# Low parts of streamed weights made by ScalarE and an accumulating GpSimd DMA instead of a VectorE subtraction

## The chip, the cores and the metric

One Trainium2 chip; the kernel runs on 1 core, so there is one span and one granted TensorE clock per run. The metric is the device time of one execution in microseconds (us). Times are medians of several executions; the profile is one further execution with a time of its own.

## The reference, cut to what matters

Two layers of a decoder trunk on 512 tokens of 1024 features. Each layer is an FFN half-step, a mixer, and another FFN half-step; layer 0 has the indexed sparse attention (mixer A), layer 1 the gated MLP (mixer B).

```python
def swiglu(x, w_in, w_out):
    gate, up = jnp.split(x @ w_in, 2, axis=-1)
    return (jax.nn.silu(gate) * up) @ w_out
...
    for i in range(DEPTH):
        kind, j = i % N_MIXERS, i // N_MIXERS
        h = h + 0.5 * swiglu(rmsnorm(h, norm_g[i, 0]), ffn_w_in[i, 0], ffn_w_out[i, 0])
        hn = rmsnorm(h, norm_g[i, 1])
        if kind == 0:
            y = mixer_a(hn, a_w_in[j], a_w_out[j], rel_table)
        elif kind == 1:
            y = mixer_b(hn, b_w_in[j], b_b_in[j], b_ln_g[j], b_ln_b[j], b_w_sp[j], b_b_sp[j], b_w_out[j])
```

D_MODEL is 1024, D_FF 2816, and mixer B's inner width 3072. Everything is float32, about 200 MB of weights are read once (the last FFN's output weights partly twice), and each weight is used for all 512 tokens.

## The kernel before, in words

**Precision by splitting.** TensorE multiplies in the fp32r format. To keep float32 accuracy every operand is a sum of a high part (rounded to fp32r) and a low part (what is left). A product of weight and activation is three matmuls into one PSUM bank (`mul3`, lines 217 to 219): high weight by high activation, high weight by low activation, low weight by high activation. The low weight is thus first needed by the third matmul of a piece.

**The weight stream.** A piece is one 128x128 block of weights. All pieces lie in DRAM in the order of their use, eight to a load of 512 KB (`in_wst`). `WeightStream` keeps three queues going. `_load_to` starts loads on the SP queue into four `raw` buffers. `_convert_to` takes four pieces (a conversion): ScalarE (ACT) copies `raw` into `whi` (line 92), and `lo_engine` writes `wlo = raw - whi` (line 93). `lo_engine` is VectorE (DVE) as a rule; while DVE is busy with a row of small dependent operations, the code sets it to GpSimd (POOL): in the first FFN from its third column pair to its seventh, and in the middle of mixer A. `take` hands out pieces and first asks for conversions up to AHEAD = 5 conversions ahead, each in one of 6 buffers. `background` holds small DVE tasks, some of which are started after each conversion.

**The order of work.** There is no scheduler. Each engine runs its instructions in the order in which the code is written and waits on semaphores, so an instruction that waits holds all that stand behind it on the same engine. DMAs issued by POOL go into one queue (q0 in the profile), those by SP into another (q1).

**The stages.** An FFN first multiplies by `ffn_w_in` (`group` for the first four column blocks, then `single` for one block at a time), forms `yh` and `yl` on ACT and DVE, and then multiplies by `ffn_w_out` and adds to `H`. In the first FFN the hook `behind(k)` prepares the next block of activations after every four pieces (ACT writes `xh` and a square, POOL adds the square to `sqacc`). After the fourth block it also calls `bias_rows`: TensorE makes a small table of relative position biases, DVE copies it to `rows`, and POOL issues one DMA that writes 2560 KB of copies of it to DRAM (`dist`, line 339). Mixer A reads them later (`tb`). At its start mixer B loads `bias`, `wT`, `bs` and three small vectors by POOL DMAs, and POOL masks `wT` when it has landed (line 627). In the last FFN the output columns come in two halves of 256 tokens, so each weight is used by matmuls of half the width and the weights pass twice as fast. While the second half runs, POOL normalizes the first half (`hg`, line 792) and issues its four output DMAs.

Of the kernel before, what the change touches and what calls it, by code (L numbers as in the profile page):

```python
# [12 lines left out]
F32 = mybir.dt.float32  # L13
F32R = mybir.dt.float32r
I32 = mybir.dt.int32
AF = mybir.ActivationFunctionType
ALU = mybir.AluOpType
PSUM = bass.MemoryType.PSUM

P = 128  # L20
D = 1024
S = 512
# [20 lines left out]
CONV = 4  # L43
LOAD = 8
# [3 lines left out]
SPACE = 8  # L48


class WeightStream:

    AHEAD = 5
    LOADS_AHEAD = 3

    def __init__(self, nc, pool, dram):
# [24 lines left out]

    def _convert_to(self, n):
        while self.converted < min(n, N_PIECES // CONV):
            c = self.converted
            i, part = divmod(c * CONV, LOAD)
            self._load_to(i + self.LOADS_AHEAD + (part > 0))
            src = self.raw[i][:, part * P:(part + CONV) * P]
            hi = self.pool.tile([P, CONV * P], F32R, tag="whi", bufs=self.AHEAD + 1, name=f"whi{c}")  # L90
            lo = self.pool.tile([P, CONV * P], F32R, tag="wlo", bufs=self.AHEAD + 1, name=f"wlo{c}")
            self.nc.scalar.activation(hi, src, AF.Copy)  # L92
            self.lo_engine.tensor_tensor(lo, src, hi.bitcast(F32), op=ALU.subtract)  # L93
            self.conv[c] = (hi, lo)
            self.conv.pop(c - self.AHEAD - 1, None)
            self.converted += 1
            for _ in range(min(self.pops, len(self.background))):
                self.background.pop(0)()

    def take(self, *specs):  # L100
        at = len(self.specs)
        c, off = divmod(at, CONV)
        assert off + len(specs) <= CONV
        self._convert_to(c + min(self.AHEAD, c + 1))
        self.specs += specs
# [10 lines left out]
def tile_trunk(ctx: ExitStack, tc, specs_out, xT, wst, gT, rel, onehot, bu, bv, lng, lnb, wspT, bsp, out):  # L116
# [12 lines left out]
    def uname(s):  # L129
        counter[0] += 1  # L130
        return f"{s}_{counter[0]}"
# [106 lines left out]
    def split(src, hi, lo):  # L238
        nc.scalar.activation(hi, src, AF.Copy)  # L239
        nc.vector.tensor_tensor(lo, src, hi.bitcast(F32), op=ALU.subtract)  # L240

    def ffn(layer, which, finish, hooks=None, parts=1):


        NJ = DFF // P
        half = NJ // 2
        with tc.tile_pool(name=uname("ffn"), bufs=1) as fp:

            def spec_in(k, c):
# [2 lines left out]
            def activate(psg, psu, rb):  # L252
                gs = fp.tile([P, S], F32, tag="gs", bufs=2, name=uname("gs"))
                us = fp.tile([P, S], F32, tag="us", bufs=2, name=uname("us"))
                sg = fp.tile([P, S], F32, tag="sg", bufs=2, name=uname("sg"))
                a = fp.tile([P, S], F32, tag="a", bufs=2, name=uname("a"))
                nc.vector.tensor_tensor(gs, psg, rb, op=ALU.mult)
                nc.scalar.activation(sg, gs, AF.Silu)
                nc.vector.tensor_tensor(us, psu, rb, op=ALU.mult)
                nc.vector.tensor_tensor(a, sg, us, op=ALU.mult)  # L260
                yh = fp.tile([P, S + SPACE], F32R, tag="yh", bufs=half + 1, name=uname("yh"))[:, :S]
                yl = fp.tile([P, S + SPACE], F32R, tag="yl", bufs=half + 1, name=uname("yl"))[:, SPACE // 2:S + SPACE // 2]
                split(a, yh, yl)
                return yh, yl

# [5 lines left out]
            for hf in range(2):  # L271
# [10 lines left out]
                def activate_one():  # L282
                    if pend and rb[0] is not None:
                        Y.append(activate(*pend.pop(0), rb[0]))

                for p in range(p0 + len(pend), p0 + half):
                    tag = "aux" if (p // 2) % 2 else "acc"
# [20 lines left out]
                for at in range(0, S, n):  # L308
                    s = slice(at, at + n)
# [433 lines left out]
    with tc.tile_pool(name="bias", bufs=1) as bp:  # L743
        table, dist = load_table(), []
        ffn(0, 0, into(1), {k: lambda k=k: behind(k) for k in range(KD)})
    mixer_a(dist[0], 2)
    ffn(0, 1, into(3))
    ffn(1, 0, into(4))
    mixer_b(5)

# [101 lines left out]
```

## Time and profile before

| what | value |
| --- | --- |
| time, median of 3 executions | 2156.6 us (2156.14 to 2157.45) |
| the profiled execution's own time | 2156.59 us |
| its span, first to last instruction | 2154.8 us |
| mean granted TensorE clock | 0.998 |
| TensorE (PE) busy | 2135.0 us, 99% |
| VectorE busy | 1141.3 us, 53% |
| ScalarE busy | 752.8 us, 35% |
| GpSimd busy | 131.9 us, 6% |

The profiled execution stands at the median, and its span is 1.8 us shorter than its time. The engines work beside each other, so the busy times do not add up; a busy PE row says that matmuls follow each other without a gap, not how fast they are.

### The profile page before, as it was taken

The numbers are of one execution on the slowest core, as the hardware profiler recorded it, in microseconds if no ns is written. First come the engines' busy times: TensorE is split into PE (matmuls) and PEld (weight loads), VectorE is DVE, ScalarE is ACT, GpSimd is POOL, SyncE is SP. The second block draws the span as 40 slices with busy tenths as digits, with TensorE's granted clock in tenths as the row PEclk, the third lists the DMA queues.
The fourth block names the chain that finished last, engine by engine and source line by source line (L and its number), as shares of the span: only waits on it lengthen the run. The fifth ranks groups of instructions, "written<-read, shape, count | busy, mean of one in ns | idle before, by whom it ended". The sixth has DMA issues, their size and how long they took to land.

```text
span 2154.8 us, 25553 instructions
## 1 busy us (share of the span) xinstructions
PE 2135.0 (99%) x9816; PEld 1768.0 (82%) x9816; DVE 1141.3 (53%) x1968; ACT 752.8 (35%) x1317; POOL 131.9 (6%) x122
## 2 busy tenths in 40 slices
PE   8999999999999999999999999999999999999998
PEld 7788888888888888888888888888888888888888
DVE  6443444696656434445543444555846466533456
ACT  4322333444443322333332333333423243322344
POOL 3300000143200000000000000000000000000002
PEclk9999999999999999999999999999999999999999
DMA  6532223232122332223322232422222223222234
GB/s 181 133 98 97 94 94 98 83 108 83 60 88 98 98 98 94 95 87 107 99 97 89 98 98 88 148 88 90 97 89 91 85 88 108 97 91 96 98 123 132
DMA packets 60426, 214.67 MB, mean 100 GB/s; under 512 B 7232, under 2 KB 8320, under 8 KB 60176
## 3 DMA queue, kind: packets, MB, share of 16 engines
q1 hardware_dynamic: 57136, 203.97, 29.0%
q0 software_dynamic: 2624, 8.54, 1.9%
q8 instruction: 77, 1.26, 0.2%
q10 hardware_dynamic: 544, 0.52, 0.1%
q14 instruction: 45, 0.37, 0.1%
HBM read 208.29 MB, written 4.72 MB: 99 GB/s over the span
## 4 chain that ended last, share of the span: by engine, by line
PE 95%; DMA 3%; issue 1%; POOL 1%; DVE 0%; ACT 0%; POOLq 0%; SPq 0%; ACTq 0%
PE acc L217 16%; PE acc L219 16%; PE acc L218 16%; PE aux L219 12%; PE aux L217 12%; PE aux L218 12%; DMA raw<-in_wst 2%; PE aux L636 1%; PE aux L638 1%; PE acc L638 1%; PE acc L636 1%; PE aux L637 1%; PE acc L637 1%; PE aux L688 1%; PE acc L556 1%
## 5 line engine op out<-in xcount | busy, mean ns | idle before, releaser
L92 ACT ACTIVATE whi<-raw 128x512 fp32r<-128x512 f32 x768 | 466.6, 626 | 752.7 <-PE acc L218 357.0
L93 DVE TENSOR_TENSOR wlo<-raw,whi 128x512 fp32r<-128x512 f32 x698 | 474.5, 700 | 448.7 <-ACT whi L92 448.5
L217 PE MATMUL acc<-xh,whi 128*128 128x512 f32 x1048 | 417.9, 399 | 7.5 <-ACT xh L174 6.5
L219 PE MATMUL acc<-xh,wlo 128*128 128x512 f32 x1048 | 408.9, 390 | 0.6 <-POOL wlo L93 0.6
L218 PE MATMUL acc<-xl,whi 128*128 128x512 f32 x1048 | 408.8, 390 | 0.0
L217 PE MATMUL aux<-xh,whi 128*128 128x512 f32 x720 | 280.2, 389 | 0.9 <-ACT whi L92 0.9
L219 PE MATMUL aux<-xh,wlo 128*128 128x512 f32 x720 | 280.2, 389 | 0.6 <-POOL wlo L93 0.6
L218 PE MATMUL aux<-xl,whi 128*128 128x512 f32 x720 | 280.1, 389 | 0.0
L217 PEld LDWEIGHTS acc<-xh,whi 128*128 128x128 f32 x1048 | 197.3, 188 | 50.1 <-ACT xh L174 6.5
L219 PEld LDWEIGHTS acc<-xh,wlo 128*128 128x128 f32 x1048 | 197.0, 188 | 42.4 <-POOL wlo L93 1.1
L218 PEld LDWEIGHTS acc<-xl,whi 128*128 128x128 f32 x1048 | 197.3, 188 | 41.9 <-issue 1.4
L217 PEld LDWEIGHTS aux<-xh,whi 128*128 128x128 f32 x720 | 135.2, 188 | 29.4 <-ACT whi L92 1.4
L219 PEld LDWEIGHTS aux<-xh,wlo 128*128 128x128 f32 x720 | 135.2, 188 | 29.1 <-POOL wlo L93 1.1
L218 PEld LDWEIGHTS aux<-xl,whi 128*128 128x128 f32 x720 | 135.2, 188 | 28.2
L219 PE MATMUL aux<-yh,wlo 128*128 128x512 f32 (+1 forms) x396 | 146.3, 370 | 0.0
L219 PE MATMUL acc<-yh,wlo 128*128 128x512 f32 (+1 forms) x396 | 146.3, 369 | 0.0
L217 PE MATMUL aux<-yh,whi 128*128 128x512 f32 (+1 forms) x396 | 146.0, 369 | 0.0
L217 PE MATMUL acc<-yh,whi 128*128 128x512 f32 (+1 forms) x396 | 146.0, 369 | 0.0
L218 PE MATMUL acc<-yl,whi 128*128 128x512 f32 (+1 forms) x396 | 145.7, 368 | 0.0
L218 PE MATMUL aux<-yl,whi 128*128 128x512 f32 (+1 forms) x396 | 145.7, 368 | 0.0
L93 POOL TENSOR_TENSOR wlo<-raw,whi 128x512 fp32r<-128x512 f32 x70 | 93.4, 1347 | 166.6 <-ACT whi L92 120.5
L240 DVE TENSOR_TENSOR yl<-a,yh 128x512 fp32r<-128x512 f32 x88 | 62.5, 710 | 61.5 <-ACT yh L239 61.5
(211 smaller groups left out, 2559.0 us busy)
## 6 DMA issues: line engine op xcount, KB each, us to landing
raw<-in_wst SPq DMA_DIRECT2D x383, 512.0 KB, 3.4
dist<-rows POOLq DMA_DIRECT2D x1, 2560.0 KB, 57.0
h<-in_xT SPq DMA_DIRECT2D x8, 256.0 KB, 6.6
tb<-dist POOLq DMA_DIRECT2D x8, 256.0 KB, 3.4
bias<-in_bv POOLq DMA_DIRECT2D x1, 1536.0 KB, 7.2
out<-hg POOLq DMA_DIRECT2D x4, 256.0 KB, 3.3
raw<-in_wst SPq DMA_DIRECT2D x2, 256.0 KB, 3.6
wT<-in_wspT POOLq DMA_DIRECT2D x1, 512.0 KB, 8.2
```

The lines of the kernel that those rows point to most:

```text
L92: self.nc.scalar.activation(hi, src, AF.Copy)
L93: self.lo_engine.tensor_tensor(lo, src, hi.bitcast(F32), op=ALU.subtract)
L217: mm(ps, wh, xh, start=first, stop=False)
L218: mm(ps, wh, xl, start=False, stop=False)
L219: mm(ps, wl, xh, start=False, stop=last)
L240: nc.vector.tensor_tensor(lo, src, hi.bitcast(F32), op=ALU.subtract)
L556: mm(po[0][:, b * P:(b + 1) * P], V[j][:, h * P:(h + 1) * P], pT[:, j * P:(j + 1) * P], start=j == 0, stop=j == b)
L636: mm(banks[t], xh, wh, start=k == 0, stop=False)
L637: mm(banks[t], xl, wh, start=False, stop=False)
L638: mm(banks[t], xh, wl, start=False, stop=k == KD - 1)
L688: mm(ps[:, t * P:(t + 1) * P], V[t][:, d * P:(d + 1) * P], wT[:, g, :], start=True, stop=True)
```

## The change

A unit is now a whole load of eight pieces, converted at once, and AHEAD is 4 conversions. Where `lo_engine` was DVE, ACT writes the high part and also its negative (a copy with scale -1, rounded alike) into `low`, twice each for a unit. Then POOL issues one DMA that reads the same 512 KB of weights from DRAM a second time and adds them to `low` in SBUF, which leaves weight minus high part. Where `lo_engine` is POOL, the subtraction stays on POOL, two instructions to a unit. There are three `low` buffers of 4 KB per partition (six of 2 KB before) and six of `whi` as before. In an FFN, `yl` moves by 128 bytes and the offsets of `yh` and `yl` inside their tiles change by 16 bytes.

```diff
-    AHEAD = 5
+    AHEAD = 4
...
     def _convert_to(self, n):
         while self.converted < min(n, N_PIECES // CONV):
-            c = self.converted
-            i, part = divmod(c * CONV, LOAD)
-            self._load_to(i + self.LOADS_AHEAD + (part > 0))
-            src = self.raw[i][:, part * P:(part + CONV) * P]
-            hi = self.pool.tile([P, CONV * P], F32R, tag="whi", bufs=self.AHEAD + 1, name=f"whi{c}")
-            lo = self.pool.tile([P, CONV * P], F32R, tag="wlo", bufs=self.AHEAD + 1, name=f"wlo{c}")
-            self.nc.scalar.activation(hi, src, AF.Copy)
-            self.lo_engine.tensor_tensor(lo, src, hi.bitcast(F32), op=ALU.subtract)
-            self.conv[c] = (hi, lo)
-            self.conv.pop(c - self.AHEAD - 1, None)
-            self.converted += 1
-            for _ in range(min(self.pops, len(self.background))):
+            i = self.converted * CONV // LOAD
+            self._load_to(i + self.LOADS_AHEAD)
+            raw = self.raw[i]
+            by_dma = self.lo_engine is self.nc.vector
...
+                low = self.pool.tile([P, LOAD * P], F32R, tag="wlo", bufs=self.AHEAD // 2 + 1, name=f"wlo{i}")
+            for part in range(0, LOAD, CONV):
+                c = self.converted
+                s = slice(part * P, (part + CONV) * P)
+                hi = self.pool.tile([P, CONV * P], F32R, tag="whi", bufs=self.AHEAD + 2, name=f"whi{c}")
+                self.nc.scalar.activation(hi, raw[:, s], AF.Copy)
+                if by_dma:
+                    self.nc.scalar.activation(low[:, s], raw[:, s], AF.Copy, scale=-1.0)
+                else:
+                    self.lo_engine.tensor_tensor(low[:, s], raw[:, s], hi.bitcast(F32), op=ALU.subtract)
+                self.conv[c] = (hi, low[:, s])
+                self.conv.pop(c - self.AHEAD - 1, None)
+                self.converted += 1
+            if by_dma:
+                self.nc.gpsimd.dma_start(low, self.dram[i], accum_op=ALU.add)
+            for _ in range(min(2 * self.pops, len(self.background))):
                 self.background.pop(0)()
...
-                yh = fp.tile([P, S + SPACE], F32R, tag="yh", bufs=half + 1, name=uname("yh"))[:, :S]
-                yl = fp.tile([P, S + SPACE], F32R, tag="yl", bufs=half + 1, name=uname("yl"))[:, SPACE // 2:S + SPACE // 2]
+                at = slice(SPACE // 2 * which, S + SPACE // 2 * which)
+                yh = fp.tile([P, S + SPACE], F32R, tag="yh", bufs=half + 1, name=uname("yh"))[:, at]
+                if not padded:
+                    padded.append(fp.tile([P, 32], F32, name=uname("pad_y")))
+                yl = fp.tile([P, S + SPACE], F32R, tag="yl", bufs=half + 1, name=uname("yl"))[:, at]
```

How instructions move is shown at three places. The first is POOL in the first FFN, around the `dist` DMA. Before:

```order
L322 DMA oh_sb<-in_onehot 32x640
L186 TENSOR_TENSOR sqacc_159<-sqacc_159,sq_183 128x512
L186 TENSOR_TENSOR sqacc_159<-sqacc_159,sq_210 128x512
L186 TENSOR_TENSOR sqacc_159<-sqacc_159,sq_237 128x512
L339 DMA dist<-rows 1024x1x640
L186 TENSOR_TENSOR sqacc_159<-sqacc_159,sq_281 128x512
```

And in the changed kernel (line numbers shift by some 15; `wlo<-in_wst` is the accumulating DMA of one unit):

```order
L107 DMA wlo_165<-in_wst 128x1024
L197 TENSOR_TENSOR sqacc_163<-sqacc_163,sq_187 128x512
L107 DMA wlo_192<-in_wst 128x1024
L197 TENSOR_TENSOR sqacc_163<-sqacc_163,sq_214 128x512
L107 DMA wlo_219<-in_wst 128x1024
L197 TENSOR_TENSOR sqacc_163<-sqacc_163,sq_241 128x512
L354 DMA dist<-rows 1024x1x640
L197 TENSOR_TENSOR sqacc_163<-sqacc_163,sq_275 128x512
L107 DMA wlo_280<-in_wst 128x1024
L197 TENSOR_TENSOR sqacc_163<-sqacc_163,sq_302 128x512
L197 TENSOR_TENSOR sqacc_163<-sqacc_163,sq_319 128x512
L107 DMA wlo_324<-in_wst 128x1024
```

Before `dist` stand the DMAs of units 0 to 3 (unit 0's is above the rows shown), and units 4, 5 and 6 follow it in the same queue; unit 6's is two rows further on, and from unit 7 on POOL subtracts.

The second place is the start of ACT. Before:

```order
L154 ACTIVATE ones_r<-ones 128x128
L92 ACTIVATE whi_125<-raw_99 128x512
L174 ACTIVATE xh_80<-h_71,g_sb 128x512
L174 ACTIVATE xh_81<-h_72,g_sb 128x512
L182 ACTIVATE sqacc_159<-h_71 128x512
L92 ACTIVATE whi_161<-raw_99 128x512
```

And in the changed kernel:

```order
L165 ACTIVATE ones_r<-ones 128x128
L98 ACTIVATE whi_126<-raw_99 128x512
L100 ACTIVATE wlo_125<-raw_99 128x512
L98 ACTIVATE whi_129<-raw_99 128x512
L100 ACTIVATE wlo_125<-raw_99 128x512
L185 ACTIVATE xh_80<-h_71,g_sb 128x512
L185 ACTIVATE xh_81<-h_72,g_sb 128x512
```

One conversion stood ahead of the first `xh`; now four ACT instructions do, and the accumulating DMA of unit 0 waits for the fourth.

The third place is the end of POOL, in the last FFN's second half of tokens. Before, POOL ran there:

```order
L792 TENSOR_TENSOR hg<-hg,last_rb_16577 128x256 x2
L795 DMA out<-hg 128x2x256
L792 TENSOR_TENSOR hg<-hg,last_rb_16577 128x256 x2
L795 DMA out<-hg 128x2x256
L792 TENSOR_TENSOR hg<-hg,last_rb_16904 128x256 x3
```

And in the changed kernel:

```order
L107 DMA wlo_16522<-in_wst 128x1024
L807 TENSOR_TENSOR hg<-hg,last_rb_16544 128x256 x2
L810 DMA out<-hg 128x2x256
L807 TENSOR_TENSOR hg<-hg,last_rb_16544 128x256 x2
L810 DMA out<-hg 128x2x256
L807 TENSOR_TENSOR hg<-hg,last_rb_16544 128x256 x2
L810 DMA out<-hg 128x2x256
L807 TENSOR_TENSOR hg<-hg,last_rb_16544 128x256 x2
L810 DMA out<-hg 128x2x256
L107 DMA wlo_16579<-in_wst 128x1024
L107 DMA wlo_16619<-in_wst 128x1024
```

The eight `hg` operations and four output DMAs now stand ahead of the accumulating DMAs of the last six units. In the same way the six loads of mixer B and the masking of `wT` stand ahead of the DMA of mixer B's third unit.

## Rows read from the trace of the kernel before

**Rows 1.** The page, part 1: busy us, share of the span, instructions.

```profile
PE 2135.0 (99%) x9816; PEld 1768.0 (82%) x9816; DVE 1141.3 (53%) x1968; ACT 752.8 (35%) x1317; POOL 131.9 (6%) x122
```

**Rows 2.** The page, part 4: the chain that ended last, by engine.

```profile
PE 95%; DMA 3%; issue 1%; POOL 1%; DVE 0%; ACT 0%; POOLq 0%; SPq 0%; ACTq 0%
```

**Rows 3.** Costliest groups: the conversion; count, busy us, mean ns, idle before.

```profile
L92 ACT ACTIVATE whi<-raw 128x512 fp32r<-128x512 f32 x768 | 466.6, 626 | 752.7 <-PE acc L218 357.0
L93 DVE TENSOR_TENSOR wlo<-raw,whi 128x512 fp32r<-128x512 f32 x698 | 474.5, 700 | 448.7 <-ACT whi L92 448.5
```

**Rows 4.** Windows: busy us and instructions by engine, granted clock, DMA share, GB/s.

```profile
core 0: us, PE busy (x) PEld busy (x) DVE busy (x) ACT busy (x) POOL busy (x), PEclk, DMA share, GB/s
...
10.00:15.00 5.00, 5.00 (x23) 4.16 (x22) 4.65 (x6) 4.38 (x9) 2.85 (x2) 1.00 1.04 398
...
55.00:85.00 30.00, 26.78 (x115) 20.78 (x114) 13.50 (x17) 11.60 (x21) 15.32 (x11) 1.00 0.57 131
85.00:135.00 50.00, 50.00 (x222) 41.41 (x221) 25.64 (x39) 17.04 (x28) 2.88 (x2) 1.00 0.34 116
...
1900.00:1950.00 50.00, 50.00 (x218) 40.61 (x217) 17.59 (x27) 12.32 (x21) 0.00 (x0) 1.00 0.30 96
...
2080.00:2110.00 30.00, 30.00 (x255) 30.00 (x254) 19.95 (x38) 17.83 (x37) 0.00 (x0) 1.00 0.55 175
```

**Rows 5.** DMA issues, whole span: KB each, median us from issue to landing.

```profile
raw<-in_wst SPq DMA_DIRECT2D x383, 512.0 KB, 3.4
dist<-rows POOLq DMA_DIRECT2D x1, 2560.0 KB, 57.0
...
tb<-dist POOLq DMA_DIRECT2D x8, 256.0 KB, 3.4
wT<-in_wspT POOLq DMA_DIRECT2D x1, 512.0 KB, 8.2
...
bu_sb<-in_bu POOLq DMA_DIRECT2D x1, 12.0 KB, 9.6
```

**Rows 6.** Timeline, first 32 us: start, duration, idle before.

```profile
3.50 0.63 ACT L92 ACTIVATE whi<-raw 128x512 fp32r<-128x512 f32 x1 [1.08 <-DMA raw<-in_wst]
...
7.86 0.63 PE L219 MATMUL acc<-xh,wlo 128*128 128x512 f32 x1
...
8.28 0.63 PE L217 MATMUL acc<-xh,whi 128*128 128x512 f32 x1
...
9.99 0.43 PE L218 MATMUL acc<-xl,whi 128*128 128x512 f32 x1
...
21.10 1.09 POOL L339 DMA_DIRECT2D dist<-rows  x1 [3.48 <-DVE rows L337]
...
31.58 0.39 PE L219 MATMUL aux<-xh,wlo 128*128 128x512 f32 x1
```

**Rows 7.** Waits between 60 and 85 us: total us, times, longest.

```profile
ACT whi L92 <- DMA raw<-in_wst: 13.4, 3, 4.5
```

**Rows 8.** Timeline of POOL at mixer B's start.

```profile
1358.39 0.55 POOL L620 DMA_DIRECT2D bias<-in_bv  x1 [755.59 <-PE aux L219]
...
1367.42 1.40 POOL L627 TENSOR_SCALAR_AFFINE_SELECT wT<-wT 128x1024 f32<-128x1024 f32 x1 [5.61 <-DMA wT<-in_wspT]
```

**Rows 9.** Costliest groups: VectorE at the column ends of mixer B's first part.

```profile
L653 DVE SCALAR_TENSOR_TENSOR z<-acc,rcol,bias 128x512 f32<-128x512 f32 x12 | 8.9, 739 | 4.6 <-PE acc L638 4.5
```

**Rows 10.** Groups of ACT from 2080 to 2142 us.

```profile
L762 ACT ACTIVATE hg<-h,g_sb 128x256 f32<-128x256 f32 x15 | 7.4, 494 | 0.0
L185 ACT ACTIVATE sq<-h 128x256 f32<-128x256 f32 x12 | 5.0, 418 | 20.9 <-DVE h L313 20.9
```

**Rows 11.** Timeline of POOL near the end.

```profile
2120.43 1.88 POOL L792 TENSOR_TENSOR hg<-hg,last_rb 128x256 f32<-128x256 f32 x2 [751.61 <-ACT last_rb L786]
...
2131.51 0.75 POOL L795 DMA_DIRECT2D out<-hg  x1 [0.30 <-POOL hg L792]
```

**Rows 12.** Waits, whole span: ACT in mixer B's second part.

```profile
ACT u L680 <- DVE u L679: 67.9, 23, 5.8
```

More of the change, by code (lines that the diff above doesn't have):

```diff
@@ L85, in _convert_to @@
         while self.converted < min(n, N_PIECES // CONV):
-            c = self.converted
-            i, part = divmod(c * CONV, LOAD)
-            self._load_to(i + self.LOADS_AHEAD + (part > 0))
-            src = self.raw[i][:, part * P:(part + CONV) * P]
-            hi = self.pool.tile([P, CONV * P], F32R, tag="whi", bufs=self.AHEAD + 1, name=f"whi{c}")
-            lo = self.pool.tile([P, CONV * P], F32R, tag="wlo", bufs=self.AHEAD + 1, name=f"wlo{c}")
-            self.nc.scalar.activation(hi, src, AF.Copy)
-            self.lo_engine.tensor_tensor(lo, src, hi.bitcast(F32), op=ALU.subtract)
-            self.conv[c] = (hi, lo)
-            self.conv.pop(c - self.AHEAD - 1, None)
-            self.converted += 1
-            for _ in range(min(self.pops, len(self.background))):
+            i = self.converted * CONV // LOAD
[5 more added lines that the diff above has]
+            else:
+                low = self.pool.tile([P, LOAD * P], F32R, tag="wlo", bufs=self.AHEAD // 2 + 1, name=f"wlo{i}")
+            for part in range(0, LOAD, CONV):
[5 more added lines that the diff above has]
+                    self.nc.scalar.activation(low[:, s], raw[:, s], AF.Copy, scale=-1.0)
+                else:
+                    self.lo_engine.tensor_tensor(low[:, s], raw[:, s], hi.bitcast(F32), op=ALU.subtract)
+                self.conv[c] = (hi, low[:, s])
+                self.conv.pop(c - self.AHEAD - 1, None)
+                self.converted += 1
+            if by_dma:
+                self.nc.gpsimd.dma_start(low, self.dram[i], accum_op=ALU.add)
+            for _ in range(min(2 * self.pops, len(self.background))):
                 self.background.pop(0)()
@@ L246, in ffn @@
         half = NJ // 2
+        padded = []
         with tc.tile_pool(name=uname("ffn"), bufs=1) as fp:
```

## The prediction

> **What bounds the kernel now.** I read the page's busy times first: PE is busy for 2135.0 us, 99% of the span, every other engine for about half of it or less [rows 1]. The chain that ended last says the same, 95% PE [rows 2]. So the kernel is bound by the rate of matmuls, and two things alone can change its time: the step from one matmul to the next, and gaps in PE.
>
> The windows give the step [rows 4]: 222 matmuls in 50 us with weights against `xh` and `xl`, 0.225 us each; 218 in 50 us with `yh` and `yl`, 0.229; 255 in 30 us in the last half-width stage, 0.118. A unit of eight pieces is 24 matmuls, so PE uses up a unit in 5.4 us, in the last stage in 2.8 us. These two numbers are what every supply of weights has to meet. The only gap inside the run that one window shows is 30.00 - 26.78 = 3.2 us between 55 and 85 us [rows 4]. There ACT waited three times for a `raw` load, up to 4.5 us [rows 7], while the `dist` DMA was under way from 21.10 us for 57.0 us [rows 5, 6].
>
> The subtraction on DVE does not hold PE: it takes 474.5 us of an engine that is idle for half of the span [rows 1, 3]. Taking it off DVE is worth nothing by itself; the sum below is of what the new route costs.
>
> **The price of the new route.** For each unit ACT does four copies of 0.63 us, 2.5 us instead of 1.3 [rows 3]; with 752.8 us busy now and some 698 copies more it stays near 55%. POOL issues one DMA per unit. No accumulating DMA is in the trace. Its low bound from issue to landing is 4.0 us: the 256 KB POOL loads land in 3.4 us [rows 5], and the other 256 KB cost 0.7 us at the 398 GB/s that the engines reached between 10 and 15 us [rows 4]. Its far bound is the rate of `dist`, 57.0 us for 2560 KB, so 11.4 us for 512 KB. I take 5.3 us, near the loads of the same form: 3.4 us for a 512 KB load, 1.3 us more because the old content of `low` has to be read too, and 0.6 us for sharing with the `raw` load that the same ACT copy sets free. The Trainium skill, DMA: Bandwidth & Descriptors, section Anatomy of one DMA, fits a POOL-issued copy as 2.0 us plus bytes over 436 GB/s, 3.2 us for this size; it has no price for an addition, and by 3.2 us the time below would come out some 10 us lower.
>
> **Steady state: hidden.** A `low` buffer is free when PE ends a unit, and is needed two units, 10.8 us, later (and 0.45 us after that, as the low part is the third matmul). Until then ACT does three of the four copies (the first needs only half a unit), 1.9 us, and the DMA takes 5.3: 7.2 us. The cover is 4.1 us. It is the same in the input part of every FFN and wherever nothing holds ACT or POOL. Where POOL still subtracts, it has two subtractions to a unit as now, and I count nothing. The cover is gone at five places.
>
> **1. The first FFN.** ACT now does four copies before the first `xh`: from 3.50 us on [rows 6] that is 6.0 us, and the DMA engines are full at that time (share 1.04 between 10 and 15 us), so I let unit 0 land at 12.5 us (bounds 10.0 and 13.2). The third matmul moves from 7.86 to 12.5 us, 4.6 us late. All behind it moves alike, so POOL issues `dist` at 25.7 us instead of 21.10, and it lands 57.0 us later, at 82.7 us. The DMAs of units 4, 5 and 6 stand behind it in the same queue. What that means is shown at mixer B's start: `bu_sb`, 12 KB, issued behind `bias`, `wT` and `bs`, took 9.6 us, and `wT`, 512 KB, 8.2 us instead of 3.4 [rows 5]. The queue is worked off in order. So unit 4's low part lands after `dist` and its own transfer of two times 1.3 us: 85.2 us. Before, the same matmul ran at 31.58 us [rows 6]. That is 53.6 us. The 3.2 us gap goes, since `dist` is over when the weights flow again. After so long a pause the matmuls restart slowly: from 7.86 to 9.99 us five steps took 0.43 us each instead of 0.225 [rows 6], about 1.2 us. First FFN: **+51.6 us**.
>
> **2. Mixer B's start.** POOL's mask of `wT` waits until `wT` has landed and ends at 1367.42 + 1.40, 10.4 us after the loads were issued [rows 8]. The DMA of the third unit from there stands behind it on POOL: 10.4 + 5.3 = 15.7 us, needed at 11.3. **+4 us** (0 to 6).
>
> **3. Column ends of mixer B's first part.** ACT's four Gelu copies wait for DVE's four `z` of 0.74 us [rows 9], about 3.6 us, and then come four weight copies and the DMA: 3.6 + 2.5 + 5.3 = 11.4 against 11.3. **+1 us** over the five ends that have work behind them (0 to 7).
>
> **4. The half-width stage.** A unit lasts 2.8 us. A buffer goes round in 1.9 + 5.3 + 2.8 = 10.0 us, three buffers, so 3.3 us per unit. There are 22 units (176 pieces): 22 x 0.5 = 11, less the two units made ahead: **+9 us**. Lower bound 6: ACT alone needs per unit four copies and, for 8 of a column's 11 pieces, 0.7 of `hg` 0.494 and `sq` 0.418 [rows 10], 3.2 us. Upper bound 25: three passes of 512 KB per unit at 398 GB/s are 3.95 us.
>
> **5. POOL near the end.** From 2120.43 to 2132.3 us POOL normalizes and sends the first half [rows 11], 12 us, and the DMAs of the last six units wait behind it on POOL. PE has some 2.2 units ahead, 6 us; a unit lands 5.3 us after POOL is free. **+10 us** (6 to 12).
>
> The move of `yl` I count as nothing. It touches the 1848 full-width matmuls with `yh` and `yl`; their step can at best fall to the 0.225 of the others, 8 us, and I see no row for a sign. DVE's release is nothing too: the window with the busier DVE (25.64 of 50 us) has the shorter step than the one with 17.59 [rows 4].
>
> Sum: 51.6 + 4 + 1 + 9 + 10 = 75.6. The profiled execution's own time is 2156.59 us, which is the median of the others; so **2232 us**, and all but the places above as before.
>
> **Rivals.**
> *Not queued behind `dist`.* If the accumulating DMAs pass it, place 1 shrinks to the late start and some 5 us of sharing engines with `dist`, as the `raw` loads do now: 2232 - 51.6 + 4.6 + 5 = 2190 us. For it: no accumulating DMA is in the trace. Against: the landings of [rows 5]. The Trainium skill, DMA: Bandwidth & Descriptors, section Queues, rings and completion order, has each engine consume the descriptors of one ring in order and alternate only between rings; `bu_sb` agrees, and by that rule this rival falls away.
> *A dear addition.* At 8 us from issue to landing mixer B's second part stalls: there ACT waits 3.0 us per turn for `u` [rows 12], then follow a Gelu copy, four weight copies (3.2 us) and the DMA, 14.2 us against two turns of 12. That decides from about 6 us on. 24 turns of 2 us, 13 us in place 3, 22 in place 4, 3 each in places 1 and 2: 2232 + 89 = 2321 us. At the far bound of 11.4 us in every unit the DMA queue would be the bound, with thousands of us; only the form of `dist` speaks for that.
> *Faster.* If DVE's 698 subtractions held up PE's reads of SBUF, so that the step falls everywhere, 0.01 us over 9816 matmuls is 98 us; from 0.0077 us on it outweighs everything above, and at 0.0085 us the time is 2149. Against it stand the two windows with busier DVE and shorter step.
>
> **How the numbers follow.** The forecast with its five places 0.60, its own range 2213 to 2255; not queued 0.13; dear addition 0.16; faster 0.08; no change in sum 0.03. The range 2185 to 2300 leaves out the faster cases and the dearer half of the dear ones, about 2 in 10. What counts as a change is 0.2%, about what three executions of this kernel tell apart. Faster 0.08, same 0.03, slower 0.89.
>
> **What would show it.** In the changed profile: one gap of PE of 45 to 50 us ending near 85 us with `wlo<-in_wst` as releaser; landings of 50 us for the two or three DMAs behind `dist` and a median near 5 us; PE without gaps from 100 to 1360 us; a gap of 4 us near mixer B's start; fewer than 255 matmuls per 30 us in the last stage, and a gap of some 10 us behind `hg`. A landing of unit 4 well before `dist` makes the prediction wrong, as does a median landing above 6 us, or a step other than 0.225 us in the long stretches.

## The result and the profile after

The changed kernel takes 2361.69 us (median of 4, 2360.51 to 2366.39) against 2156.94 for the kernel before in the same comparison: ratio 1.0954, interval 1.0935 to 1.0973, 205 us slower. The direction was forecast, the size was not: 2232 was forecast, and 2300 was the end of the range. The profiled execution was the slowest of the four, 2366.39 us, so what is read from its trace adds up to some 4 us more.

The busy times of the profiled execution of the changed kernel (answers to [rows 1]):

```profile
PE 2186.5 (92%) x9816; PEld 1799.5 (76%) x9816; DVE 705.6 (30%) x1270; ACT 1104.1 (47%) x2015; POOL 424.5 (18%) x471
```

The same 9816 matmuls keep PE busy for 51.5 us longer than before, and PE is idle for 178.1 us of the span of 2364.6 instead of 19.8. DVE is relieved by 436 us, which buys nothing. What PE waited for (total us, times, longest):

```profile
PE aux L230 <- DMA wlo<-in_wst: 80.7, 12, 48.7
PE acc L230 <- DMA wlo<-in_wst: 36.1, 11, 6.9
PE acc L653 <- DMA wlo<-in_wst: 16.5, 3, 8.5
PE aux L653 <- DMA wlo<-in_wst: 11.0, 3, 3.9
```

In 29 waits, 144.3 us, PE stood at a low part that the accumulating DMA had not yet delivered. Ten more waits at a low part, 14.2 us, the profile puts down to ScalarE's copies; in the trace the DMA of the unit landed 0.13 to 0.14 us before the matmul started in those too. The DMA queues (packets, MB, share of 16 engines) and issues (count, KB, median us to landing; answers to [rows 5]):

```profile
q0 software_dynamic: 52880, 191.54, 45.2%
q1 hardware_dynamic: 57136, 203.97, 29.9%
...
raw<-in_wst SPq DMA_DIRECT2D x383, 512.0 KB, 6.1
wlo<-in_wst POOLq DMA_DIRECT2D x349, 512.0 KB, 7.6
dist<-rows POOLq DMA_DIRECT2D x1, 2560.0 KB, 56.8
```

The accumulating DMA lands after 7.6 us where 5.3 was taken, and a `raw` load now takes 6.1 us instead of 3.4. (Beside a plain copy of the same bytes it takes 3.5, see plain_copy below, so it is the addition that slows it.)

Where the time builds up is seen by comparing when the same matmul of the weight stream starts in both traces. Units count from 0; the table gives the start in the changed kernel minus that in the kernel before, in us, for unit 50 (the dist stall is over), 235 (mixer B begins), 259 (its first part ends), 307 (mixer B ends), 362 (the half-width stage begins) and the last matmul with streamed weights:

| kernel | unit 50 | 235 | 259 | 307 | 362 | last |
| --- | --- | --- | --- | --- | --- | --- |
| changed kernel | 55.9 | 85.4 | 126.4 | 147.3 | 148.4 | 208.5 |
| forecast | 51.6 | 51.6 | 56.6 | 56.6 | 56.6 | 75.6 |

So the first place came near the forecast (55.9 us for 51.6), mixer B's first part and the half-width stage cost a multiple of theirs, and the stretches from unit 50 to 235 and from 259 to 307, where nothing was forecast, cost 29.5 and 20.9 us.

### The profile page after: what moved, and what is told of

Its sections match the earlier page's. It is cut to its first block, busy times and chain, and to the rows that moved or that the text cites. A ratio compares the mean times of both kernels' runs of the same rounds, so it can differ in the third digit from the quotient of the medians.

```text
span 2364.6 us, 26231 instructions
## 1 busy us (share of the span) xinstructions
PE 2186.5 (92%) x9816; PEld 1799.5 (76%) x9816; DVE 705.6 (30%) x1270; ACT 1104.1 (47%) x2015; POOL 424.5 (18%) x471
## 3 DMA queue, kind: packets, MB, share of 16 engines
q0 software_dynamic: 52880, 191.54, 45.2%
q1 hardware_dynamic: 57136, 203.97, 29.9%
## 5 line engine op out<-in xcount | busy, mean ns | idle before, releaser
L100 ACT ACTIVATE wlo<-raw 128x512 fp32r<-128x512 f32 x698 | 433.7, 621 | 452.0 <-PE acc L230 187.7
L107 POOL DMA_DIRECT2D wlo<-in_wst x349 | 298.1, 858 | 1689.3 <-ACT wlo L100 1569.2
L98 ACT ACTIVATE whi<-raw 128x512 fp32r<-128x512 f32 x768 | 473.1, 620 | 253.5 <-ACT wlo L100 103.0
L230 PEld LDWEIGHTS acc<-xh,wlo 128*128 128x128 f32 x1048 | 197.5, 188 | 54.1 <-DMA wlo<-in_wst 8.2
L230 PE MATMUL acc<-yh,wlo 128*128 128x512 f32 (+1 forms) x396 | 152.2, 384 | 25.8 <-DMA wlo<-in_wst 20.5
L229 PE MATMUL acc<-yl,whi 128*128 128x512 f32 (+1 forms) x396 | 150.6, 380 | 0.0
## 6 DMA issues: line engine op xcount, KB each, us to landing
bias<-in_bv POOLq DMA_DIRECT2D x1, 1536.0 KB, 10.1
```

Source lines behind the costliest of these rows:

```text
L98: self.nc.scalar.activation(hi, raw[:, s], AF.Copy)
L100: self.nc.scalar.activation(low[:, s], raw[:, s], AF.Copy, scale=-1.0)
L107: self.nc.gpsimd.dma_start(low, self.dram[i], accum_op=ALU.add)
L229: mm(ps, wh, xl, start=False, stop=False)
L230: mm(ps, wl, xh, start=False, stop=last)
```

## The experiments

**Theory.** An accumulating DMA of a whole unit takes longer than I priced it and starts only behind four ScalarE copies, so the cover is gone wherever ScalarE or GpSimd is held. **Rivals.** The coarser units with a shorter lead; ScalarE's doubled copies; any second read through GpSimd's queue, added or not.

**unit8_dve: units of eight without the new route.**

```diff
-            by_dma = self.lo_engine is self.nc.vector
+            by_dma = False
```

> The changed kernel with its units of eight pieces, AHEAD of 4 and moved yl, but VectorE subtracts as before: no negated copies by ScalarE, no accumulating DMA. Theory (the route over the DMA costs the time: what it adds from issue to landing, 7.6 us against the 5.3 us I took, and its place behind dist): about the time before, 2150 to 2165 us, since a subtraction is done 0.7 us after the copy. Rival (the coarser units with one conversion less made ahead cost it, whoever makes the low part): 2250 us or more, with gaps of PE at the column ends and in the half-width stage as in the changed kernel.

2159.71 us, ratio 1.0015 (1.0006 to 1.0025). The units, AHEAD of 4 and the moved `yl` cost 3.5 us together, with VectorE subtracting; units as such fall away as the cause of 205.

**no_dma: the four copies without the DMA.**

```diff
-            if by_dma:
-                self.nc.gpsimd.dma_start(low, self.dram[i], accum_op=ALU.add)
```

> The changed kernel without the accumulating DMA: the low part stays the negated high part, so the product lacks the weights that the DMA would add. It keeps ScalarE's four copies per unit, and takes away the whole DMA. Theory (the DMA costs the time): a few us over the time before, 2160 to 2175 us, all of it in the half-width stage, where ScalarE needs some 3.2 us per unit against 2.8. Rival (ScalarE's doubled copies cost it): 2300 us or more, with ScalarE as what ends PE's waits at the column ends.

2157.37 us, ratio 1.0006 (0.9996 to 1.0016), with no wait of PE for ScalarE in the half-width stage either. Better than the theory had it: without a DMA behind them ScalarE's copies are free. This is also about the best that the route could reach here if its DMA were free, and it is no faster than before, though VectorE is released.

**plain_copy: the DMA writes instead of adding.**

```diff
-                self.nc.gpsimd.dma_start(low, self.dram[i], accum_op=ALU.add)
+                self.nc.gpsimd.dma_start(low, self.dram[i])
```

> The changed kernel with the same DMA per unit, but it writes the weights over the negated high part instead of adding them, so the low part is the whole weight. It takes away the price of the addition alone; queue, waits, size and place stay. Theory (two things: the addition makes a packet about 2.4 times as long as a copy's, and the queue behind dist): landing near 4.5 us, the stall behind dist stays at about 50 us, and most of the other 150 us go: 2215 to 2245 us. Rival (any second read of the weights through GpSimd's queue costs it, by the issue, the descriptors or the shared engines): landing stays above 7 us and the time above 2320 us.

2278.6 us, ratio 1.0568 (1.0552 to 1.0584): between the two theories. Its queue and issues:

```profile
q0 software_dynamic: 52880, 191.54, 24.0%
...
raw<-in_wst SPq DMA_DIRECT2D x383, 512.0 KB, 3.5
wlo<-in_wst POOLq DMA_DIRECT2D x349, 512.0 KB, 4.5
```

With the same packets q0's share falls from 45.2% to 24.0%. q0's other work is 1.9% of 2156.0 us x 16 = 655 us (the queue's row without the DMA). So a unit takes (0.452 x 2364.6 x 16 - 655) / 349 = 47 us of engine time when it adds and (0.240 x 2276.6 x 16 - 655) / 349 = 23 us when it copies, an estimate from these shares. The addition doubles the engines' time (the expectation had 2.4 times) and accounts for 83 of the 205 us. But a copy that lands in 4.5 us, less than I had taken, still loses 122 us: 53.4 up to unit 50 and 66.4 behind it, where the sum had 24. The landing alone was not the error.

**dist_act: dist by another queue.**

```diff
-        nc.gpsimd.dma_start(d, rows.unsqueeze(1).broadcast_to([HEADS, P, TBW]))
+        nc.scalar.dma_start(d, rows.unsqueeze(1).broadcast_to([HEADS, P, TBW]))
```

> The changed kernel with the dist DMA issued by ScalarE, so in another queue than the accumulating DMAs, at the same place in the program. Theory (units 4 to 6 wait because they stand behind dist in one queue): the gap of 49 us that ends near 89 us goes, a few us of sharing engines stay: 2310 to 2325 us. Rival (dist holds the DMA engines themselves, whatever the queue): unit 4 lands no earlier and the time stays above 2350 us.

2339.04 us, ratio 1.0845 (1.0824 to 1.0865): a gain of 23, less than half of the stall, so neither theory. Up to unit 50 it still loses 35.3 us, the longest wait being 18.7 us. The issues from 30 to 95 us:

```profile
raw<-in_wst SPq DMA_DIRECT2D x6, 512.0 KB, 22.2
...
wlo<-in_wst POOLq DMA_DIRECT2D x3, 512.0 KB, 29.6
```

Out of the queue, unit 4's DMA landed 25.8 us after its issue, at 61.2 us, while packets of `dist` ran until 92.3 us. So the queue's order had held it in the changed kernel, where it took 56.9 us. But the weights then share engines with `dist`, and even the `raw` loads need 22.2 us.

**dist_later: dist while GpSimd subtracts.** The DMA goes out where `lo_engine` becomes GpSimd, which lasts longer.

```diff
                         W.lo_engine = nc.gpsimd
+                        late.pop()()
...
-                    elif p == 6:
+                    elif p == 9:
...
-        nc.gpsimd.dma_start(d, rows.unsqueeze(1).broadcast_to([HEADS, P, TBW]))
+        late.append(lambda: nc.gpsimd.dma_start(d, rows.unsqueeze(1).broadcast_to([HEADS, P, TBW])))
```

> The changed kernel with the dist DMA issued where GpSimd begins to subtract in the first FFN, and GpSimd subtracting up to the tenth column pair instead of the seventh, so that no accumulating DMA is queued behind dist or shares the engines with it. Theory (place 1 is dist alone): the first FFN costs under 8 us instead of 55.6, all else stays: 2308 to 2320 us. Rival (part of the 55 us is the accumulating DMA's own weakness at the start): still 25 us or more at the end of the first FFN's first half.

2312.69 us, ratio 1.0733 (1.0709 to 1.0758), in the theory's range; 10.3 us at unit 50, where under 8 was expected, nearly all of it unit 0's late landing (9.9 us at unit 4).

**quad_dma: units of four.** The kernel before, with one DMA of 256 KB per conversion:

```diff
-            self.lo_engine.tensor_tensor(lo, src, hi.bitcast(F32), op=ALU.subtract)
+            if self.lo_engine is self.nc.vector:
+                self.nc.scalar.activation(lo, src, AF.Copy, scale=-1.0)
+                self.nc.gpsimd.dma_start(lo, self.dram[i, :, part * P:(part + CONV) * P], accum_op=ALU.add)
```

> The kernel before (units of four pieces, five conversions ahead, six buffers, its yl) with ScalarE's negated copy and one accumulating DMA of 256 KB per conversion. Theory (the time from issue to landing and the engines' time for the addition decide, not the size of a unit): the addition of the same bytes costs the DMA engines as much, a DMA of half the size lands some 1.5 us earlier, so the stalls outside the first FFN shrink by a third or so: 2290 to 2330 us, dist stall included. Rival (the coarse units are what makes the addition late): the stalls outside the first FFN nearly vanish, 2220 us or less.

2273.18 us, ratio 1.0539 (1.0524 to 1.0553): below the theory's range and above the rival's. The dist stall stays (55.5 us at unit 50), what follows falls from 153 to 60 us. Size and lead were changed together; two_halves separates them.

**low_late: the low matmuls at the end of a column.**

```diff
         for k in range(K):
-            mul3(ps, W.take(spec(k, c)), parts(k), k == 0, k == K - 1)
+            (wh, wl), (xh, xl) = W.take(spec(k, c)), parts(k)
+            mm(ps, wh, xh, start=k == 0, stop=False)
+            mm(ps, wh, xl, start=False, stop=False)
+            lows.append((wl, xh))
+        for k, (wl, xh) in enumerate(lows):
+            mm(ps, wl, xh, start=False, stop=k == K - 1)
```

> The changed kernel with the matmuls of the low weights at the end of each column in every stage that takes one column at a time: the low part is needed 14 to 20 matmuls later, 3 to 4 us, the work of every engine and DMA stays. Theory (two limits: outside the half-width stage a late landing of 7.6 us, in the half-width stage the DMA engines' own time per unit, some 4.5 us against 2.8): stalls of FFN output columns and of mixer A's output go, about 30 us, the half-width stage keeps most of its 60: 2310 to 2335 us. Rival (lateness alone, everywhere): the half-width stage loses 40 us or more too, under 2295 us. Rival (throughput everywhere): 2350 us or more.

2337.19 us, ratio 1.0837 (1.0822 to 1.0852), 2 us above the theory's range. The half-width stage still costs 52 us. The patience there was less than expected: the first piece of a column is needed 20 matmuls of 0.118 us later, 2.4 us, and the last piece no later at all. So the run fits a supply rate that is missing in this stage, and does not prove it.

**before_split: the kernel before with dist in two halves.**

```diff
-        nc.gpsimd.dma_start(d, rows.unsqueeze(1).broadcast_to([HEADS, P, TBW]))
+        def send(n):
+            s = slice(n * P // 2, (n + 1) * P // 2)
+            nc.gpsimd.dma_start(d[:, s], rows.unsqueeze(1).broadcast_to([HEADS, P // 2, TBW]))
+        send(0)
+        late.append(lambda: send(1))
...
                     elif p == 6:
+                        if late:
+                            late.pop()()
```

> The kernel before with the dist DMA sent as two halves of 64 copies, the second at the seventh column pair of the first FFN. Theory (dist slows the raw loads by sharing DMA engines, until their lead of three loads is used up): the 3.2 us of gaps between 60 and 85 us go, 2152.5 to 2154 us against 2156.2. Rival (those gaps are from another cause): no difference.

2152.03 us, ratio 0.9982 (0.9973 to 0.9991): faster than both kernels, and 0.5 us under the theory's range. Each half lands in 29.7 us, and ScalarE's waits for `raw` [rows 7] are gone from the waits between 55 and 85 us.

**two_halves: the DMA of a unit in two.**

```diff
                     self.nc.scalar.activation(low[:, s], raw[:, s], AF.Copy, scale=-1.0)
+                    self.nc.gpsimd.dma_start(low[:, s], self.dram[i, :, s], accum_op=ALU.add)
```

> The changed kernel with the accumulating DMA of each unit sent as two of 256 KB, each right behind ScalarE's copies of its four pieces. Units of eight, the three low buffers and the work of the engines stay, and the DMA engines' time per unit stays near 47 us over all sixteen. Theory A (the size of one DMA made the units of four cheaper: half of it lands 1.5 us earlier and starts 1.3 us earlier): outside the first FFN the loss falls from 153 us towards the 60 us of the units of four, 2265 to 2295 us. Theory B (it was the buffers: a buffer of four pieces is free again after half a unit, and there are six): 2330 us or more.

2275.57 us, ratio 1.0551 (1.0532 to 1.0570). Theory A: the units of eight with their three buffers do as well as quad_dma. Its queue and issues:

```profile
q0 software_dynamic: 103136, 191.56, 51.8%
raw<-in_wst SPq DMA_DIRECT2D x383, 512.0 KB, 5.7
wlo<-in_wst POOLq DMA_DIRECT2D x698, 256.0 KB, 6.6
```

The engines work more than in the changed kernel (51.8% of the span, by the same estimate 52 us a unit, not the 47 expected), a half lands only 1.0 us earlier, but it starts behind two copies instead of four: the earlier start and the shorter DMA together gain 86 us.

**hg_dve: the first half's normalization off GpSimd.**

```diff
-                if end and j not in (0, 3, 6):
+                if not end or j not in (0, 3, 6):
...
-                    queue = nc.gpsimd if not end else nc.sync if j % 4 == 1 else nc.scalar
+                    queue = nc.scalar if not end else nc.sync if j % 4 == 1 else nc.scalar
```

> The changed kernel with the normalization of the first half of tokens on VectorE and its four output DMAs issued by ScalarE, so that GpSimd issues accumulating DMAs without a pause near the end. Theory (place 5: the DMAs wait on GpSimd for 10 us, and PE for 8.5): 2349 to 2354 us, and the gap of 8.5 us goes. Rival (the DMA engines are the limit there and only catch up in that pause): within 3 us of the changed kernel, 2359 us or more.

2356.61 us (2350.80 to 2361.09), ratio 1.0936 (1.0917 to 1.0956), between the two theories, and its interval overlaps the changed kernel's: inconclusive. In its trace the gap of 8.5 us shrinks to 5.5 and the stage costs 54.1 instead of 60.1 us.

**dve_hard: VectorE in two stages.** A flag, set in mixer B's first part and in the last FFN's second output half, turns `by_dma` off.

```diff
-            by_dma = self.lo_engine is self.nc.vector
+            by_dma = self.lo_engine is self.nc.vector and not self.subtract
...
+                W.subtract = n < S
```

> The changed kernel with VectorE subtracting in two stages only: mixer B's first part and the second half of the last FFN's output; everywhere else ScalarE's copy and the accumulating DMA. Theory (the loss is local: 53 us in mixer B's first part, 60 us in the half-width stage): both go but for some 5 us each at their starts, 2255 to 2265 us. Rival (stalls only move on, since the DMA queue is behind): above 2290 us.

2271.84 us, ratio 1.0537 (1.0520 to 1.0554), 7 us over the theory's range: mixer B's first part now costs nothing (90.1 us at unit 235, 90.0 at 259), the half-width stage 1.2 us. The losses are local.

**repaired: units of four, dist later, VectorE in the two stages.** The edits of quad_dma, dist_later and dve_hard together.

> Units of four with an accumulating DMA each as before in this study, dist sent while GpSimd subtracts (up to the tenth column pair), and VectorE subtracting in mixer B's first part and in the last FFN's second output half. Theory (the five places are all there is, and they add up): 2273 us less 50 for dist, 15 for mixer B's first part, 33 for the half-width stage: 2170 to 2182 us. In no case under the kernel before, since without any DMA the route gave 2157 us; a time under 2154 us would show a gain from VectorE's release.

2175.70 us, ratio 1.0088 (1.0072 to 1.0104), as expected. The places add up, and the route still loses 19 us; in the profile 9.5 of them arise in mixer B's second part.

**bn_after: VectorE's order at a column end.** The trace of the changed kernel shows VectorE and ScalarE at a column end of mixer B's first part in turns (start, duration, idle before):

```profile
1506.18 0.75 DVE L668 SCALAR_TENSOR_TENSOR z<-aux,rcol,bias 128x512 f32<-128x512 f32 x1 [19.88 <-PE aux L653]
1507.63 0.69 DVE L671 BATCH_NORM_STATS2 stats<-bv 128x6 f32<-128x512 f32 x1 [0.70 <-ACT bv L670]
1508.24 0.73 DVE L668 SCALAR_TENSOR_TENSOR z<-aux,rcol,bias 128x512 f32<-128x512 f32 x1
...
1513.10 0.63 ACT L670 ACTIVATE bv<-z 128x512 f32<-128x512 f32 x1 [1.41 <-DVE z L668]
1513.64 0.61 ACT L98 ACTIVATE whi<-raw 128x512 fp32r<-128x512 f32 x1
...
1516.11 0.84 POOL L107 DMA_DIRECT2D wlo<-in_wst  x1 [10.45 <-ACT wlo L100]
```

Each `bn_stats` waits for the Gelu copy of its own column and holds up the next `z`. From the first `z` to the end of the fourth Gelu copy pass 7.5 us, and the DMA is issued 9.9 us after the column ended.

```diff
                         nc.scalar.activation(V[t][:, sl], z, AF.Gelu_apprx_tanh)
-                        nc.vector.bn_stats(stats[:, t, c, :], V[t][:, sl])
+                    for t in range(NT):
+                        nc.vector.bn_stats(stats[:, t, c, :], V[t][:, c * 512:(c + 1) * 512])
```

> The changed kernel with the four bn_stats of a column of mixer B's first part behind all four of its z operations on VectorE instead of one behind each. Nothing else moves. Theory (place 3: ScalarE is held 7.5 us at a column end since each z waits for a bn_stats that waits for the Gelu copy before it; without that the hold is near the 3.6 us that I took): the five gaps of 3.4 to 4.4 us shrink to under 1 us, with the slow matmuls behind them 20 to 28 us less: 2333 to 2342 us. Rival (the DMAs of three units at once are what is late, whenever ScalarE begins): the gaps stay above 2.5 us and the time above 2350 us.

2330.98 us, ratio 1.0813 (1.0795 to 1.0831), a gain of 31, more than expected. Its trace at a column end:

```profile
1499.18 2.88 DVE L668 SCALAR_TENSOR_TENSOR z<-aux,rcol,bias 128x512 f32<-128x512 f32 x4 [16.07 <-PE aux L653]
...
1499.96 2.77 ACT L670 ACTIVATE bv<-z 128x512 f32<-128x512 f32 x4 [2.46 <-DVE z L668]
```

The four Gelu copies now end 3.6 us after the first `z` began, the very figure that the forecast had taken, and no wait for a low part above 0.5 us is left behind the one at mixer B's start. (At that column end the low part was needed 13.2 us after the first `z`, where place 3 had 11.3; that margin makes up for most of the longer landing.) The gain is in the clock as well. The windows from behind mixer B's first stall to the end of its first part (columns as in [rows 4]), first the changed kernel, with its half-width stage below, then bn_after:

```profile
1464.00:1640.00 176.00, 153.62 (x613) 123.38 (x614) 40.35 (x74) 70.59 (x125) 20.43 (x24) 0.92 0.63 146
...
2232.00:2349.00 117.00, 76.76 (x499) 74.51 (x499) 14.15 (x40) 51.81 (x107) 25.50 (x32) 0.82 0.76 171
```

```profile
1466.00:1606.00 140.00, 139.52 (x614) 114.56 (x612) 39.17 (x75) 71.69 (x125) 20.46 (x24) 0.99 0.80 178
```

The same number of matmuls (613 and 614) takes 153.6 us at a mean granted clock of 0.92 and 139.5 us at 0.99. Of the 36 us between the stretches 22 are six gaps of 3.4 to 4.4 us and 14 are slower matmuls behind them, at the lower of TensorE's two levels (1.2 GHz; the mean of 0.92 mixes it with 2.4).

**halves_copy: two_halves, writing instead of adding.** `accum_op=ALU.add` is left out.

> Units of eight with two DMAs of 256 KB that write the weights over the negated high part instead of adding them, so the low part is the whole weight; compared with the same two DMAs that add, 2275.6 us, of which 41 us arise in the half-width stage. Theory (in that stage the DMA engines' own time for an addition is the limit once the DMAs are small: share 0.87 there): its 41 us fall to under 20, the stall behind dist stays at some 53, the rest falls to under 10: 2225 to 2240 us. Rival (lateness by the DMA's fixed time is the limit there): the stage keeps 30 us or more, above 2245 us.

2243.75 us, ratio 1.0406 (1.0391 to 1.0422), 4 us over the theory's range; the half-width stage costs 21.2 us, 8.0 of them in one gap behind `hg`. Its issues:

```profile
q0 software_dynamic: 103136, 191.56, 30.2%
raw<-in_wst SPq DMA_DIRECT2D x383, 512.0 KB, 3.9
wlo<-in_wst POOLq DMA_DIRECT2D x698, 256.0 KB, 4.1
```

With landings of 4.1 us and a start behind two copies the table comes near the forecast: 51.0 at unit 50, 53.3 at 235, 61.6 at 259, 62.4 at 362 and 83.6 at the end, where 75.6 was forecast.

## Why the prediction was wrong in size

Two terms of the sum failed: the price of the DMA, 5.3 us, which was 7.6; and the holds of ScalarE in front of its copies, which the sum put at nothing outside mixer B's first part and at 3.6 us there, and which are 2.4 to 10.1 us. Together they use up the cover of 4.1 us.

**1. The first FFN: right, with too low a price for sharing.** The changed kernel's timeline:

```profile
16.20 0.79 PE L230 MATMUL acc<-xh,wlo 128*128 128x512 f32 x1 [6.87 <-DMA wlo<-in_wst]
...
29.90 1.15 POOL L354 DMA_DIRECT2D dist<-rows  x1 [2.78 <-DVE rows L352]
...
32.28 0.92 POOL L107 DMA_DIRECT2D wlo<-in_wst  x1
...
89.21 0.80 PE L230 MATMUL aux<-xh,wlo 128*128 128x512 f32 x1 [48.69 <-DMA wlo<-in_wst]
```

Unit 0 landed at 16.2 instead of 12.5 us, so `dist` went out at 29.9 instead of 25.7, and unit 4 came at 89.2 instead of 85.2: one gap of 48.7 us, released by `wlo<-in_wst`, and 55.9 us in all where 51.6 was forecast. The order in one queue holds. The rule of the Trainium skill on one ring (DMA: Bandwidth & Descriptors, section Queues, rings and completion order) agrees with the trace here, and unit 4 landed behind `dist`. The rival "not queued" would have paid more than it claimed: in another queue (dist_act) sharing the engines costs some 26 us beside unit 0's lateness, not the 5 I gave it. The trace of the kernel before had shown that: of its `raw` loads, in another queue than `dist`, the six issued from 23 to 66 us landed after 20.6 to 31.5 us,

```profile
raw<-in_wst SPq DMA_DIRECT2D x6, 512.0 KB, 26.0
```

and PE lost only 3.2 us there, as loads are started three ahead.

**The price: a failed step.** "I take 5.3 us" was 7.6. The term for the addition was 1.3 us, a second pass at the rate of a copy; measured side by side it is 3.1 us (7.6 against 4.5). The fit of the Trainium skill for a POOL-issued copy (same page, section Anatomy of one DMA), 3.2 us for this size, is below what the copy took beside the `raw` loads, 4.5 us; it has no price for the addition. The range of 4.0 to 11.4 held 7.6, and I gave a price near it a chance of 0.16. By my own steady state, a unit then takes 2.0 us from the release of its buffer to the issue and 7.6 us to the landing (which counts POOL's issuing): 9.6 of 11.3 us. The trace agrees: over units 25 to 49 the low part landed 1.65 us in the mean before it was needed, not 4.1. That still suffices where nothing interferes (no stall between units 20 and 50).

**The holds of ScalarE: the other failed step.** "It is the same in the input part of every FFN and wherever nothing holds ACT or POOL" was true, but "gone at five places" missed most of the places where ACT is held. Where nothing holds it, its first negated copy starts 0.09 us after the buffer is free (units 25 to 49). In front of every stall between units 50 and 309 but the one at mixer B's start, 24 in all, it starts 2.4 to 10.1 us after. The stall of unit 62, at a column end of the first FFN's output:

```profile
406.02 0.72 ACT L185 ACTIVATE xh<-h,g_sb 128x512 fp32r<-128x512 f32 x1 [4.36 <-DVE h L328]
...
407.69 0.61 ACT L100 ACTIVATE wlo<-raw 128x512 fp32r<-128x512 f32 x1
...
416.34 0.47 PE L230 MATMUL acc<-yh,wlo 128*128 128x512 f32 x1 [2.07 <-DMA wlo<-in_wst]
```

The buffer was free at 402.5 us, but `xh` stood ahead of the copies on ACT and waited for VectorE's `h`; the DMA landed at 416.2. The second halves of the FFN outputs and the end of mixer A make up 27 of the 29.5 us between units 50 and 235, which I had at zero. In mixer B's second part, 20.9 us, two stalls in its output cost 14.5 and the sixth column end of the first part, which falls behind unit 259, 5.2. The turns with `u`, from which the rival "a dear addition" took 48 us and its bound of 6 us, cost 1.2: its sum of 2321 came nearer than mine, but not for its main reason. In no_dma the same holds cost nothing, and in plain_copy, with a landing of 4.5 us, less than half of the loss behind unit 50 is left (66.4 of 152.6 us): it takes the holds and the dear DMA together.

**2 and 3. Mixer B's first part: 41.0 us against 5.** At its start the mask of `wT` ended 14.0 us after the first of the loads was issued, not 10.4, with three units behind it; the gap is 8.5 us instead of 4. At the column ends the term "about 3.6 us" for the hold of ScalarE was wrong: I summed the `z` of [rows 9] and did not look at what stands between them; it was 7.5 us. bn_after shows it: with the hold at 3.6 us, the same dear DMA costs next to nothing at the column ends, as place 3 had it.

**4 and 5. The half-width stage: 60.1 us against 19.** With the measured 47 us a unit, and some 27 us for a `raw` load (29.9% of 2156.0 us x 16 over 383, without the DMA), the 16 engines need some 4.6 us per unit against PE's 2.8, an estimate from these shares: 40 us over 22 units, less what the lead gives, and above the 25 that I had as the upper bound for place 4. two_halves and quad_dma lose about that (41.6 and 34.9 us). quad_dma's window there shows the engines nearly full (the last but one number, the DMA share, is 0.92):

```profile
2152.00:2258.00 106.00, 81.41 (x574) 76.02 (x572) 16.45 (x44) 56.67 (x116) 44.84 (x54) 0.92 0.92 204
```

The changed kernel's share is 0.76 in its window above, so there the engines are not full. What is tight in its trace is the cycle of three buffers that place 4 had at 10.0 us. Over units 365 to 377 it takes 16.5 us in the mean: 2.3 until ScalarE starts its negated copies, 1.9 to the issue, 8.3 to the landing, and 4.0 until PE is through with the unit. That is 5.5 us a unit instead of 2.8, at that pace 59 us over 22 units. So the mechanism of place 4 was right and its terms were too small, the landing (5.3) and the hold (nothing) above all. This is argued from the trace: no run changes the number of buffers alone, and how much of the 8.3 us the full engines make is open. Without the addition two DMAs per unit lose 21.2 us in this stage (halves_copy) instead of 41.6. For place 5, the gap behind `hg` was 8.5 us, within the 6 to 12 that it gave, but taking `hg` off POOL won 5 us in the median, within the scatter.

**The slow restart was a term of 1.2 us and is one of some 50**: PE is busy for 51.5 us more than before, in no_dma, without the gaps, for 1.8 us more. I counted it for one pause only. Behind the pause of 48.7 us the granted clock was 0.57 in the window from 90 to 95 us, mostly the lower level of 1.2 GHz, with 15 matmuls in 5 us, and 1.00 with 24 matmuls in the next 5 us. But gaps of a few us bring it down too: in the half-width stage PE was busy for 76.76 us with 499 matmuls, 0.154 us each instead of 0.118 [rows 4], at a mean clock of 0.82.

**Right:** the steps of the matmuls are unchanged where nothing stalls, DVE's release and `yl` together gain nothing (no_dma), and ScalarE has room on the average. The rival "faster" did not come: no_dma releases DVE as well.

## What to carry to other kernels

A DMA that replaces an engine's pass is late by everything ahead of it: count the copies it waits for, what holds the engine that makes them, and the time from issue to landing, and send it in the smallest part that can start early; sending it in halves was worth 86 of 205 us here. A hold of an in-order engine is read between the timestamps of its first and last instruction, not summed from the durations of the operations that it waits for, and every such hold of the kernel counts, not only those that cost something before the change. What sharing engines with a long transfer costs is read from the other transfers beside it, not from the gaps that a lead has hidden. Where several small gaps are forecast for a TensorE that never paused, add the slower matmuls behind each gap; here they came to about a quarter of the loss.

## What the hardware showed that I had not expected

An accumulating DMA from DRAM into SBUF kept the DMA engines busy for twice as long as a plain one of the same packets (47 against 23 us per 512 KB, the estimates above), landed 3.1 us later, and POOL's issue took 0.86 us instead of 0.53 (the two kernels' groups of POOL). A transfer of 57 us that repeats eight rows into DRAM took up the engines so far that loads of another queue landed after 26.0 us in the median instead of 3.4, in the kernel before. Six gaps of 3.4 to 4.4 us in 176 us brought the mean granted clock to 0.92.
